# Turning the latents of an attention layer by VectorE blocks and a row exchange instead of TensorE transposes

## The chip, the cores and the metric

One Trainium2 chip; the kernel runs on one of its cores. The metric is the device time of one execution in microseconds (us). A profiled execution gives the span from the first to the last instruction of the program, and the rows that are quoted. PE is TensorE (PEld its weight loads), DVE VectorE, ACT ScalarE, POOL GpSimd, SP SyncE; a trailing q (SPq) marks the engine's instruction queue, where a DMA is issued.

## The reference, cut to what matters

Two layers of an encoder on 512 tokens of width 2048. Of the projection `z` the change touches the first 832 columns: the query latent (512), the key/value latent (256) and the shared rotary key (64).

```python
for l in range(DEPTH):                                   # 2
    h = rmsnorm(x, pre_norm_g[l])
    z = h @ w_in[l]                                      # 2048 -> 4928 columns
    q_lat, kv_lat, k_pe, gb, gc, xin, q_mem, gate = split_cols(z)   # 512, 256, 64, ...
    q  = (rmsnorm(q_lat, q_norm_g[l]) @ w_uq[l]).reshape(b, s, 8, 192)
    q  = concat(q[..., :128], apply_rope(q[..., 128:], cos, sin))
    kv = (rmsnorm(kv_lat, kv_norm_g[l]) @ w_ukv[l]).reshape(b, s, 8, 256)
    k_nope, v = kv[..., :128], kv[..., 128:]
    k  = concat(k_nope, apply_rope(k_pe, cos, sin) for all heads)
    a_out = mla_attention(q, k, v)                       # 8 heads, softmax over 512 tokens
    c_out = short_gated_conv(gb, gc, xin, conv_w[l])
    m_out = memory_attention(q_mem, rmsnorm(mem) @ w_mk, rmsnorm(mem) @ w_mv)   # 4 heads, 256 tokens
    y = concat(a_out, c_out, m_out) * silu(gate)
    x = x + rmsnorm(y @ w_o[l], post_norm_g[l])
```

All arrays are float32.

## The kernel before, in words

**Precision.** TensorE works on float32r operands, each number split in a high and a low part; a product is three matmuls (lines 272 to 274: high by high, high by low, low by high). A weight block of 256 x 512 is loaded by a DMA into one of 8 buffers `wr` (line 146), ScalarE writes its high part `wh` (line 189), VectorE the rest `wl` (line 190). There are three buffers each for `wh` and `wl`, so the two engines are at most three blocks ahead of TensorE.

**The projection** is cut into five groups of columns. Each group is computed by Strassen's rule in seven products (P1 to P7) of halves; their weight operands are sums and differences of blocks. Sums are partly made by VectorE (line 178) and partly by the DMA: POOL issues a load that adds to a buffer already used (`accum_op=add`, line 163 by way of 146). Such a load can only be issued when VectorE has written the `wl` that was made from the buffer's earlier content, and the next `wh` of that buffer waits until it has landed.

The fourth group gives the latents. The fifth, `g4`, gives the gates of the attention heads and has 28 steps of 12 matmuls each: 0 to 3 are P1, 4 to 11 P5 and P2 in turn, 12 to 19 P6 and P3, 20 to 23 P7, 24 to 27 P4. The weight block of step 23 is that of step 19 with another block added to it by a POOL load. What follows `g4` is the mixer: rotary queries first, then the memory heads, then the eight attention heads.

**Order.** TensorE, SP and POOL run in the order in which the program is written; the order of ScalarE and VectorE is made by a scheduler when the kernel is built, and is fixed then. Every engine executes in its order, so a waiting instruction holds all behind it. Work that may be late is put in a queue of deferred functions (`pr.defer`); `pr.until` empties that queue up to a condition.

**The tokens' order.** The host permutes the tokens in x so that a 32 x 32 block transpose on VectorE (line 935) and a set of DMAs that exchange rows between partitions (`exchange`, lines 937 to 943; SBUF to SBUF, 32 partitions each, pieces of 512 bytes) turn a [tokens x columns] array into [columns x tokens] in natural order. The gates and the memory queries go that way: `y<-gm`, `y<-ga`, `y<-cy` on SP's queue and `QmL<-qm` on POOL's.

**The latents** do not. While `g4` runs, `latents_begin` (line 1044) normalises them in place (ScalarE squares, POOL takes the root, VectorE multiplies). After step 16, `latent_turn` (line 1077) is woven into the steps: four TensorE transposes (line 917) into a PSUM bank `tps`, from which ScalarE and VectorE write the high and low parts `cqH`, `cqL` and `ckv` (lines 277 and 278). There are six such groups in each layer, between steps 16 and 23. The rotary key goes by TensorE as well (`k_rope_turn`, line 1068, tiles `krps`). Queries and keys stay in the permuted order of tokens, so the product with the gate puts the result back in place with strided views (line 1268).

Of the kernel before, what the change touches and what calls it, by code (L numbers as in the profile page):

```python
# [12 lines left out]
P = 128  # L13
# [214 lines left out]
def encoder(tc, x, xt, mem, memt, positions, columns, conv_w, w_in, q_norm_g, w_uq, w_qr, kv_norm_g, w_ukv,  # L228
# [159 lines left out]
    def tables_turned():  # L388
        G["tabd"] = dram.tile([P, 2 * S], F32, name="tabd")
        for n, wide in enumerate(G.pop("wides")):  # L390
            ps = bank("tab")
            for t in range(NT):
                nc.tensor.transpose(ps[:, t * P:(t + 1) * P], wide[:, t * P:(t + 1) * P], G["ident"])
            tab = scrap("tab")
            nc.scalar.copy(tab, ps)
            nc.gpsimd.dma_start(G["tabd"][:, n * S:(n + 1) * S], tab)
# [342 lines left out]
    def projection(l):  # L739
# [40 lines left out]
        def own_lat():  # L780
            two = [slab("lat") for _ in range(2)]
            C["lat"] = [two[t // 2][:, (t % 2) * 1024:(t % 2) * 1024 + 832] for t in range(NT)]

        lat = lambda i, j, tt: C["lat"][2 * i + tt][:, j * 416:(j + 1) * 416]
        skip = lambda i, j, tt: None
# [118 lines left out]

    def mem_fetch():
        for n, k in (("Km", 4), ("Vm", 2)):
            t = slab(n, F32R)
            nc.gpsimd.dma_start(t, G[n + "d"])
            G[n] = t.rearrange("p (s i c) -> p s i c", s=2, i=k)


# [113 lines left out]
    def normalise(views, n, gain, by=None):  # L1025
        junk = scrap("junk", n)
        ssq = small(NT, "ssq4")
        for t, v in enumerate(views):
            nc.scalar.activation(junk, v, AF.Square, accum_out=ssq[:, t:t + 1])
        r = rsqrt_mean(ssq, n, NT)  # L1030
        if by:
            nc.gpsimd.tensor_scalar(r, r, by, None, op0=ALU.mult)

        def times(t, v):
            return lambda: nc.vector.scalar_tensor_tensor(v, v, r[:, t:t + 1], gain, op0=ALU.mult, op1=ALU.mult)
        for t, v in enumerate(views):
            pr.defer(0.7, times(t, v))

# [5 lines left out]
    def latents_begin(l, C):  # L1044
        G["q"] = [v[:, :QR_] for v in C["lat"]]
        G["kv"] = [v[:, O_KV:O_KV + KVR] for v in C["lat"]]
        normalise(G["q"], QR_, G["grow"][0], SC_MLA)
        normalise(G["kv"], KVR, G["grow"][1])
        pr.defer(0.0, lambda: G.update(normalised=l))

    def k_rope(C):
        m = scrap("kpm").rearrange("p (b t s i) -> p b t s i", b=2, t=NT, s=2)
        m1, m2 = m[:, 0], m[:, 1]
        for t in range(NT):
            kp = C["lat"][t][:, O_PE:O_PE + ROPE].rearrange("p (s i) -> p s i", s=2)
            nc.vector.tensor_tensor(m1[:, t], kp, G["cos2"][:, t], op=ALU.mult)
            for s in range(2):
                nc.vector.tensor_tensor(m2[:, t, s, :], kp[:, 1 - s, :], G["sin2"][:, t, s, :], op=ALU.mult)
        nc.vector.tensor_tensor(m1, m1, m2, op=ALU.add)
# [7 lines left out]

    def k_rope_turn():
        kab = slab("KAB", F32R)
        for n, src in enumerate(G["kr"]):  # L1070
            ps = bank("krps", F32R)
            for t in range(NT):
                nc.tensor.transpose(ps[:, t * P:(t + 1) * P], src[:, t].rearrange("p d i -> p (d i)"), G["identr"])
            nc.scalar.copy(kab[:, n * S:(n + 1) * S], ps.bitcast(F32))
        G["KA"], G["KB"] = kab[:, :S], kab[:, S:2 * S]

    def latent_turn(l, tag, j):
        def f():
            if j == 0:
                pr.until(lambda: G.get("normalised") == l)  # L1080
                if tag == "cq":
                    G["cq"] = tuple(slab(n, F32R).rearrange("p (k c) -> p k c", c=S) for n in ("cqH", "cqL"))
                else:
                    both = slab("ckv", F32R).rearrange("p (s k c) -> p s k c", s=2, k=2)
                    G["ckv"] = both[:, 0], both[:, 1]
            views = G["q" if tag == "cq" else "kv"]
            ps = turn4(lambda t: views[t], j)
            H, L = G[tag]
            split_to(H[:, j, :], L[:, j, :], ps)
        return f  # L1090
# [9 lines left out]
    def q_rope_steps(l, g):  # L1100
        st = {}

        def products(n):
            def f(*ops):
                if n == 0:
                    st["w"] = tuple(a.rearrange("p (k s c) -> p k s c", k=4, s=2) for a in ops[0])
                    st["ps"] = []
                hi, lo = st["w"]
                cH, cL = G["cq"]
                ps = bank("qr")  # L1110
                st["ps"].append(ps)
                for k in range(4):
                    mm3(ps, (hi[:, k, n], lo[:, k, n]), (cH[:, k, :], cL[:, k, :]), k == 0, k == 3)
            return f
# [33 lines left out]
    def qkv_steps(l, pair, st):  # L1148
# [9 lines left out]
        def fq(i):  # L1158
            def g(*ch):
# [6 lines left out]
                for j in range(4):  # L1166
                    mm3(ps, (hi[:, j, :], lo[:, j, :]), (cH[:, j, :], cL[:, j, :]), j == 0, j == 3)
                split_to(st["Q"][:, 0, i, :], st["Q"][:, 1, i, :], ps)
            return g

        def fk(i):
            def g(*ch):
# [6 lines left out]
                for j in range(2):  # L1179
                    mm3(ps, (hi[:, j, i * 256:i * 256 + P], lo[:, j, i * 256:i * 256 + P]),  # L1180
                        (cH[:, j, :], cL[:, j, :]), j == 0, j == 1)
                split_to(st["K"][:, 0, i, :], st["K"][:, 1, i, :], ps)
            return g

        def fv(b):
            def g():
# [5 lines left out]
                for i in range(2):  # L1192
                    sl = slice((2 * b + i) * P, (2 * b + i + 1) * P)
                    for j in range(2):
                        mm3(ps[:, i * 256:(i + 1) * 256].rearrange("p (h c) -> p h c", h=2),
                            (cH[:, j, sl], cL[:, j, sl]), (hi[:, j], lo[:, j]), j == 0, j == 1)
                p3 = ps.rearrange("p (i c) -> p i c", i=2)
# [5 lines left out]
    def head_iters(j, rope, src, keys, whole=False):  # L1203
# [50 lines left out]
        def av(b):  # L1254
            def g():
# [7 lines left out]
                if b == 1:  # L1263
                    y = G["ys"][j // 4][:, j % 4, :]
                    if rope is None:
                        nc.vector.tensor_tensor(y, st["o"], y, op=ALU.mult)
                    else:
                        nc.vector.tensor_tensor(in_tiles(y), of_tiles(st["o"]), in_tiles(y), op=ALU.mult)
            return g
# [47 lines left out]
    def mixer(l, C, pair2, tail):  # L1317

        (p0, rotate0, fetch0), (p1, rotate1, fetch1) = (q_rope_steps(l, g) for g in range(2))
        put(p0)  # L1320
        add(lambda: nc.scalar.activation(small(1, "ex"), C["ga0"][:, NT - 1][:, 0, :1], AF.Exp, scale=0.0))
# [201 lines left out]
    for l in range(depth):  # L1523
# [230 lines left out]
```

## Time and profile before

| | |
|---|---|
| median of 3 runs | 1458.38 us (1457.26 to 1458.82) |
| the profiled execution's own time | 1458.55 us |
| its span | 1456.8 us (1.75 us lie around it) |
| PE busy | 1441.9 us, 99% of the span |
| DVE busy, ACT busy | 1109.4 us, 870.0 us |
| granted TensorE clock | 0.998 |
| DMA | 299.48 MB, mean 206 GB/s |

A row of a group or of a timeline names the line, the engine, the operation, out<-in, the shape; then busy time or start and duration. What stands in square brackets is how long the engine was idle just before, and what ended that. In a window's row the number ahead of the last is the mean busy share of the 16 DMA engines (it can go over 1, since packets of one engine overlap); rows of DMA queues give packets, megabytes and that share; q0 is the queue of POOL's DMAs, q1 that of SP's. Layer 0's part of the change lies at 340 to 430 us of the span, layer 1's some 724 us later.

### The profile page before, as it was taken

Reading aid. Unit: us, or ns where it says so; the run is one execution under the profiler, and the core shown is the slowest. Engines: PE = TensorE matmul, PEld = TensorE weight load, DVE = VectorE, ACT = ScalarE, POOL = GpSimd, SP = SyncE. Lnnn points to the kernel's source line nnn. Section 1 sums busy time; section 2 is a strip of 40 time slices with the busy share of each in tenths; the row PEclk is TensorE's granted clock in tenths of the full one; section 3 lists DMA queues with packets and bytes.
Section 4 is the critical chain, followed back from the end, with each engine's and each line's share of the span. In section 5 each row is a group of like instructions: output and inputs, shape, how many; then the busy total and the mean of one; then the engine's idle time right before and its main releaser. Section 6 shows DMA issues by size and latency. Waiting matters only on the chain.

```text
span 1456.8 us, 19495 instructions
## 1 busy us (share of the span) xinstructions
PE 1441.9 (99%) x7008; PEld 1227.6 (84%) x7008; DVE 1109.4 (76%) x1533; ACT 870.0 (60%) x1346; POOL 288.6 (20%) x312
## 2 busy tenths in 40 slices
PE   9999999999999999999999999999999999999997
PEld 8888888899888888888898888778988888888886
DVE  5899685987678788868879666769576776788687
ACT  7856444545559688644777434454465586776543
POOL 0032303031501100311210333030325000004111
PEclk9999999999999999999999999999999999999999
DMA  9999969597976472795987999697979865129973
GB/s 368 415 260 219 232 184 205 138 204 225 242 241 175 123 252 87 142 254 137 334 292 225 233 235 213 193 173 170 204 203 243 245 173 145 31 86 162 271 160 130
DMA packets 162499, 299.48 MB, mean 206 GB/s; under 512 B 12801, under 2 KB 52257, under 8 KB 158561
## 3 DMA queue, kind: packets, MB, share of 16 engines
q0 software_dynamic: 57216, 127.49, 43.1%
q1 hardware_dynamic: 105184, 170.74, 36.5%
q8 instruction: 55, 0.90, 0.2%
q14 instruction: 44, 0.35, 0.1%
HBM read 266.05 MB, written 21.63 MB: 197 GB/s over the span
## 4 chain that ended last, share of the span: by engine, by line
PE 86%; DMA 5%; DVE 4%; issue 3%; POOL 2%; ACT 1%; SPq 0%; POOLq 0%; DVEq 0%; ACTq 0%
PE P L273 20%; PE P L274 20%; PE P L272 20%; DMA wr<-in_w_in_dram 2%; PE ptp L1250 2%; DVE wl L190 2%; POOL wr L146 1%; PE o L273 1%; PE o L272 1%; PE o L274 1%; PE sc L272 1%; PE sc L273 1%; PE sc L274 1%; DMA wr<-in_w_mv_dram 1%; PE qps L274 1%
## 5 line engine op out<-in xcount | busy, mean ns | idle before, releaser
L189 ACT CAST wh<-wr 128x1024 fp32r<-128x1024 f32 (+2 forms) x436 | 444.4, 1023 | 426.7 <-PE P L274 312.0
L190 DVE TENSOR_TENSOR wl<-wr,wh 128x1024 fp32r<-128x1024 f32 (+2 forms) x436 | 514.5, 1184 | 234.8 <-ACT wh L189 232.1
L272 PE MATMUL P<-wh,S 128*128 128x512 f32 (+1 forms) x896 | 345.4, 386 | 1.8 <-DVE qm L542 1.1
L273 PE MATMUL P<-wl,S 128*128 128x512 f32 (+1 forms) x896 | 344.3, 384 | 2.5 <-DVE wl L190 2.3
L274 PE MATMUL P<-wh,S 128*128 128x512 f32 (+1 forms) x896 | 343.8, 384 | 0.0
L272 PE MATMUL P<-wh,A 128*128 128x512 f32 (+1 forms) x656 | 252.6, 385 | 0.0
L273 PE MATMUL P<-wl,A 128*128 128x512 f32 (+1 forms) x656 | 251.7, 384 | 0.5 <-DVE wl L190 0.5
L274 PE MATMUL P<-wh,A 128*128 128x512 f32 (+1 forms) x656 | 251.5, 383 | 0.0
L146 POOL DMA_DIRECT2D wr<-in_w_in_dram x132 | 158.4, 1207 | 419.4 <-DVE wl L190 200.9
L273 PEld LDWEIGHTS P<-wl,S 128*128 128x128 f32 x896 | 168.2, 188 | 34.1 <-DVE wl L190 4.5
L272 PEld LDWEIGHTS P<-wh,S 128*128 128x128 f32 x896 | 168.2, 188 | 33.4 <-ACT wh L189 1.8
L274 PEld LDWEIGHTS P<-wh,S 128*128 128x128 f32 x896 | 168.2, 188 | 30.1
L273 PEld LDWEIGHTS P<-wl,A 128*128 128x128 f32 x656 | 123.2, 188 | 22.5 <-DVE wl L190 0.8
L274 PEld LDWEIGHTS P<-wh,A 128*128 128x128 f32 x656 | 123.1, 188 | 22.2
L272 PEld LDWEIGHTS P<-wh,A 128*128 128x128 f32 x656 | 123.1, 188 | 21.9 <-ACT og L585 0.2
L146 POOL DMA_DIRECT2D wr<-in_w_o_dram x40 | 48.3, 1255 | 299.0 <-DVE wl L190 295.2
L1237 ACT ACTIVATE P<-sc,nm 128x512 f32<-128x512 f32 (+1 forms) x96 | 59.7, 622 | 27.8 <-DVE nm L1234 27.5
L1240 ACT ACTIVATE P<-P,rec 128x512 f32<-128x512 f32 (+1 forms) x96 | 62.1, 660 | 7.0 <-DVE rec L1239 7.0
L1234 DVE TENSOR_REDUCE nm<-sc 128x1 f32<-128x512 f32 (+1 forms) x96 | 56.6, 593 | 10.1 <-PE sc L1232 9.0
L178 DVE TENSOR_TENSOR wr<-wr,wr 128x1024 f32<-128x1024 f32 (+1 forms) x36 | 42.3, 1174 | 5.8 <-DMA wr<-in_w_in_dram 5.4
L1250 PE MATMUL ptp<-identr,P 128*128 128x128 f32 x320 | 46.0, 272 | 0.3 <-ACT P L1240 0.3
L1250 PEld LDWEIGHTS ptp<-identr,P 128*128 128x128 f32 x320 | 38.0, 140 | 6.5 <-ACT P L1240 0.7
(324 smaller groups left out, 2098.9 us busy)
## 6 DMA issues: line engine op xcount, KB each, us to landing
wr<-in_w_in_dram SPq DMA_DIRECT2D x128, 512.0 KB, 5.4
wr<-in_w_in_dram POOLq DMA_DIRECT2D x108, 512.0 KB, 7.4
wr<-in_w_o_dram SPq DMA_DIRECT2D x48, 512.0 KB, 6.5
wr<-in_w_o_dram POOLq DMA_DIRECT2D x40, 512.0 KB, 7.1
wr<-in_w_in_dram SPq DMA_DIRECT2D x32, 416.0 KB, 4.0
wr<-in_w_in_dram POOLq DMA_DIRECT2D x24, 416.0 KB, 6.1
wr<-in_w_mk_dram SPq DMA_DIRECT2D x15, 512.0 KB, 8.8
wr<-in_w_mv_dram SPq DMA_DIRECT2D x15, 512.0 KB, 10.1
```

The costliest lines, as they stand in the source:

```text
L146: engine.dma_start(dst, src, **kw)
L178: nc.vector.tensor_tensor(tiles[a], tiles[a], tiles[b], op=ALU.add)
L189: pin(nc.scalar.copy(hi[:, h], src[:, h]))
L190: pin(nc.vector.tensor_tensor(lo[:, h], src[:, h], hi[:, h].bitcast(F32), op=ALU.subtract))
L272: nc.tensor.matmul(ps, ah, bh, start=first, stop=False, **kw)
L273: nc.tensor.matmul(ps, ah, bl, start=False, stop=False, **kw)
L274: nc.tensor.matmul(ps, al, bh, start=False, stop=last, **kw)
L1234: nc.vector.tensor_reduce(nmax, ps, axis=AX.X, op=ALU.max, negate=True)
L1237: nc.scalar.activation(pt, ps, AF.Exp, bias=nmax, accum_out=tot)
L1240: nc.scalar.activation(pt, pt, AF.Copy, scale=rec)
L1250: nc.tensor.transpose(ps[:, k * P:(k + 1) * P], pt[:, k * P:(k + 1) * P], G["ident"])
```

## The change

The host reorders the columns of `w_in` so that each half of the latents' group carries whole blocks: 384 latent columns and one half of the rotary key. The latents lie in two slabs `lat` in blocks of 32 columns. They are normalised as before, then turned by eight VectorE block transposes of 128 x 384 in each layer. `latents_rows_out` moves the rows: 16 DMAs from the first slab to `D1`, all on SP's queue, and 16 from the second to `D2`, half on SP's and half on POOL's, issued between steps 17 and 22 of `g4`. `latents_split` then makes the high parts in `H1`, `H2` and the low parts in place, in four pieces placed after steps 24 to 27. The six groups of TensorE transposes in each layer are gone; the eight of the rotary key stay. The rotary tables and the rotary key are written in natural order of tokens, and the product with the gate needs no strided view any more. The loads of the memory keys `Km`, of the tables and of the memory values `Vm`, formerly one after another behind step 25, are issued after step 26 (`Km`, tables) and after the first rotary product (`Vm`); in POOL's queue the exchange to `D2` comes ahead of them.

```diff
     def latents_begin(l, C):
-        G["q"] = [v[:, :QR_] for v in C["lat"]]
-        G["kv"] = [v[:, O_KV:O_KV + KVR] for v in C["lat"]]
-        normalise(G["q"], QR_, G["grow"][0], SC_MLA)
-        normalise(G["kv"], KVR, G["grow"][1])
+        a, b = C["lat"]
+        normalise([a[:, :, :12], b[:, :, :4]], QR_, G["grow"][0], SC_MLA)
+        normalise([b[:, :, 4:12]], KVR, G["grow"][1])
+        for t in range(NT):
+            for part in (a, b):
+                pr.defer(0.6, lambda t=t, part=part: blocks_turned(part[:, t, :12]))
         pr.defer(0.0, lambda: G.update(normalised=l))
+
+    def latents_rows_out(k, p, queue, C):
+        def f():
+            if k == 0 and p == 0:
+                C["D"] = slab("D1"), slab("D2")
+            exchange(C["D"][k].rearrange("p (c n) -> p c n", n=S)[:, :3], C["lat"][k][:, :, :12], queue, (p,))
+        return f
+
+    def latents_split(n, C):
+        def f():
+            if n == 0:
+                C["H"] = slab("H1", F32R), slab("H2", F32R)
+            (d1, d2), (h1, h2) = C["D"], C["H"]
+            hi, lo = ((h1[:, :768], d1[:, :768]), (h1[:, 768:1536], d1[:, 768:1536]), (h1[:, 1536:], d2[:, :512]),
+                      (h2[:, :1024], d2[:, 512:1536]))[n]
+            split_to(hi, lo.bitcast(F32R), lo)
...
-        lat = [latent_turn(l, "cq", j) for j in range(4)] + [latent_turn(l, "ckv", j) for j in range(2)] + [k_rope_turn]
-        more = [(f, []) for f in lat[:4] + [qm_split(0, C)] + lat[4:6] + [qm_split(1, C)] + lat[6:]]
-        last = weave(g4[16:], more, 1)
-        put(last[:-2])
-        add(mem_fetch)
-        add(tables_fetch)
-        put(last[-2:])
+        put(g4[16:17])
+        add(lambda l=l: pr.until(lambda: G.get("normalised") == l))
+        beside = {
+            17: [latents_rows_out(0, 0, nc.sync, C)], 18: [latents_rows_out(0, 1, nc.sync, C)],
+            19: [latents_rows_out(0, 2, nc.sync, C)], 20: [latents_rows_out(0, 3, nc.sync, C), qm_split(0, C)],
+            21: [latents_rows_out(1, 0, nc.sync, C), latents_rows_out(1, 1, nc.gpsimd, C)],
+            22: [latents_rows_out(1, 2, nc.sync, C), latents_rows_out(1, 3, nc.gpsimd, C)],
+            23: [qm_split(1, C)], 24: [latents_split(0, C)], 25: [k_rope_turn(C), latents_split(1, C)],
+            26: [mem_fetch("Km", 4), tables_fetch, latents_split(2, C)], 27: [latents_split(3, C)],
+        }
+        for n in range(17, 28):
+            put(g4[n:n + 1])
+            for f in beside[n]:
+                add(f)
```

How the instructions stand on SP, layer 0, from the exchange of the gate `gm` to the weights of the first attention heads (`w_qr`, `w_uq`, `w_ukv`). Before:

```order
L943 DMA y_3361<-gm_1834 32x4x128 x16
L146 DMA wr_3535<-in_w_qr_dram 128x1024
L146 DMA wr_3556<-in_w_uq_dram 128x4x128 x2
L146 DMA wr_3583<-in_w_ukv_dram 128x2x512
L146 DMA wr_3608<-in_w_uq_dram 128x4x128 x2
```

Now:

```order
L943 DMA y_3371<-gm_1834 32x4x128 x16
L943 DMA D_142_3475<-lat_2430 32x3x128 x12
L146 DMA wr_3529<-in_w_qr_dram 128x1024
L943 DMA D_142_3475<-lat_2430 32x3x128 x4
L146 DMA wr_3554<-in_w_uq_dram 128x4x128 x2
L943 DMA D_143_3476<-lat_2431 32x3x128 x4
L146 DMA wr_3581<-in_w_ukv_dram 128x2x512
L943 DMA D_143_3476<-lat_2431 32x3x128 x4
L146 DMA wr_3607<-in_w_uq_dram 128x4x128 x2
```

Twenty-four exchange DMAs (`D_142` is `D1`, `D_143` is `D2`) now stand between `gm` and the weights, or among them.

On ACT, layer 0, around the weight blocks of steps 22 (`wr_3274`, now `wr_3279`) to 25 (`wr_2889`) of `g4`. Before:

```order
L189 CAST wh_3537<-wr_3274 128x1024
L277 CAST cqH_3448<-tps_3528 128x512
L792 ACTIVATE ga_117_3039<-ga_117_3039 128x16x32 x2
L189 CAST wh_3559<-wr_3315 128x1024
L189 CAST wh_3585<-wr_2871 128x1024
L277 CAST ckv_3575<-tps_3576 128x512
L189 CAST wh_3611<-wr_2889 128x1024
```

Now:

```order
L189 CAST wh_3531<-wr_3279 128x1024
L791 ACTIVATE ga_117_3039<-ga_117_3039 128x16x32 x2
L277 CAST H_145_3654<-D_142_3475 128x768
L189 CAST wh_3557<-wr_3325 128x1024
L277 CAST H_145_3654<-D_142_3475 128x768
L189 CAST wh_3583<-wr_2871 128x1024
L189 CAST wh_3610<-wr_2889 128x1024
```

Though the program has the first piece of the split behind step 24, the scheduler has put its ScalarE half ahead of the weight block of step 23 (`wr_3325`).

On DVE, layer 0, where the latents are normalised beside steps 3 and 4 of `g4` (`wl_3067`, and `wl_3110`, now `wl_3117`). Before:

```order
L1035 SCALAR_TENSOR_TENSOR lat_2430<-lat_2430,r_3090,growq_3040 128x512
L190 TENSOR_TENSOR wl_3067<-wr_2942,wh_3066 128x1024
L1035 SCALAR_TENSOR_TENSOR lat_2430<-lat_2430,r_3090,growq_3040 128x512
L1035 SCALAR_TENSOR_TENSOR lat_2431<-lat_2431,r_3090,growq_3040 128x512
L190 TENSOR_TENSOR wl_3110<-wr_2871,wh_3109 128x1024
```

Now:

```order
L190 TENSOR_TENSOR wl_3067<-wr_2942,wh_3066 128x1024
L1035 TENSOR_TENSOR ssq_123_3083<-ssq_123_3083,ssq_124_3088 128x4
L1090 TENSOR_TENSOR kpm_3248<-lat_2430,cos_2692 128x4x32
L1091 TENSOR_TENSOR kpm_3248<-lat_2431,sin_2664 128x4x32
L1090 TENSOR_TENSOR kpm_3248<-lat_2431,cos_2692 128x4x32
L1041 SCALAR_TENSOR_TENSOR lat_2430<-lat_2430,r_3096,growq_3040 128x12x32 x4
L190 TENSOR_TENSOR wl_3117<-wr_2871,wh_3116 128x1024
```

A sum of two partial square sums, and four multiplications instead of three, now stand ahead of the `wl` of step 4.

More of the change, by code (lines that the diff above doesn't have):

```diff
@@ L394, in tables_turned @@
             tab = scrap("tab")
-            nc.scalar.copy(tab, ps)
+            nc.scalar.copy(in_tiles(tab), of_tiles(ps))
             nc.gpsimd.dma_start(G["tabd"][:, n * S:(n + 1) * S], tab)
@@ L780, in own_lat @@
         def own_lat():
-            two = [slab("lat") for _ in range(2)]
-            C["lat"] = [two[t // 2][:, (t % 2) * 1024:(t % 2) * 1024 + 832] for t in range(NT)]
-        lat = lambda i, j, tt: C["lat"][2 * i + tt][:, j * 416:(j + 1) * 416]
+            C["lat"] = [slab("lat")[:, :13 * P].rearrange("p (g t j) -> p t g j", t=NT, j=32) for _ in range(2)]
+        lat = lambda i, j, tt: C["lat"][j][:, 2 * i + tt]
         skip = lambda i, j, tt: None
@@ L903, in mem_reload, with mem_fetch @@
         G.setdefault("mT", []).append(two)
-    def mem_fetch():
-        for n, k in (("Km", 4), ("Vm", 2)):
+    def mem_fetch(n, k):
+        def f():
             t = slab(n, F32R)
@@ L1025, in normalise, with times @@
     def normalise(views, n, gain, by=None):
[L1026 to L1030, printed above, removed]
+        junk = scrap("junk", n).rearrange("p (g j) -> p g j", j=32)
+        gain = gain.rearrange("p (g j) -> p g j", j=32)
+        sums = []
+        for part in views:
+            ssq = small(NT, "ssq4")
+            for t in range(NT):
+                nc.scalar.activation(junk[:, :part.shape[2]], part[:, t], AF.Square, accum_out=ssq[:, t:t + 1])
+            sums.append(ssq)
+        if len(sums) == 2:
+            nc.vector.tensor_tensor(sums[0], sums[0], sums[1], op=ALU.add)
+        r = rsqrt_mean(sums[0], n, NT)
         if by:
             nc.gpsimd.tensor_scalar(r, r, by, None, op0=ALU.mult)
[L1034 to L1037, printed above, removed]
+        def times(t, v, g):
+            return lambda: nc.vector.scalar_tensor_tensor(v, v, r[:, t:t + 1], g, op0=ALU.mult, op1=ALU.mult)
+        at = 0
+        for part in views:
+            g = gain[:, at:at + part.shape[2]]
+            at += part.shape[2]
+            for t in range(NT):
+                pr.defer(0.6, times(t, part[:, t], g))
     def latents_rows(l):
@@ L1053, in k_rope @@
         m1, m2 = m[:, 0], m[:, 1]
[L1054 to L1058, printed above, removed]
+        kp = [part[:, :, 12] for part in C["lat"]]
+        for s in range(2):
+            nc.vector.tensor_tensor(m1[:, :, s], kp[s], G["cos2"][:, :, s], op=ALU.mult)
+            nc.vector.tensor_tensor(m2[:, :, s], kp[1 - s], G["sin2"][:, :, s], op=ALU.mult)
         nc.vector.tensor_tensor(m1, m1, m2, op=ALU.add)
@@ L1066, in k_rope, with k_rope_turn @@
         G["kr"] = krA, krB
[L1068 to L1077, printed above, removed]
-        def f():
[L1079 to L1089, printed above, removed]
+    def k_rope_turn(C):
+        def f():
+            G["KA"], G["KB"] = (C["H"][1][:, c * S:(c + 1) * S] for c in (2, 3))
+            for src, dst in zip(G["kr"], (G["KA"], G["KB"])):
+                ps = bank("krps", F32R)
+                for t in range(NT):
+                    nc.tensor.transpose(ps[:, t * P:(t + 1) * P], src[:, t].rearrange("p d i -> p (d i)"), G["identr"])
+                nc.scalar.copy(in_tiles(dst), of_tiles(ps.bitcast(F32)))
         return f
@@ L1112, in f @@
                 for k in range(4):
-                    mm3(ps, (hi[:, k, n], lo[:, k, n]), (cH[:, k, :], cL[:, k, :]), k == 0, k == 3)
+                    mm3(ps, (hi[:, k, n], lo[:, k, n]), (cH[k], cL[k]), k == 0, k == 3)
             return f
@@ L1264, in g @@
                     y = G["ys"][j // 4][:, j % 4, :]
[L1265 to L1268, printed above, removed]
+                    nc.vector.tensor_tensor(y, st["o"], y, op=ALU.mult)
             return g
@@ L1319, in mixer @@
         (p0, rotate0, fetch0), (p1, rotate1, fetch1) = (q_rope_steps(l, g) for g in range(2))
-        put(p0)
+        put(p0[:1])
+        add(mem_fetch("Vm", 2))
+        put(p0[1:])
         add(lambda: nc.scalar.activation(small(1, "ex"), C["ga0"][:, NT - 1][:, 0, :1], AF.Exp, scale=0.0))
@@ L1736 @@
     given = {n: np.asarray(inputs[n]) for n in _INS}
+    order = np.r_[0:384, 768:800, 384:768, 800:given["w_in"].shape[2]]
+    given["w_in"] = given["w_in"][:, :, order]
     given.update(
```

15 lines of the change are left out of this document (12 added, 3 removed).

## Prediction

> **What bounds the kernel now.** First the page's busy times, then the waits of PE.
>
> ```profile
> PE 1441.9 (99%) x7008; PEld 1227.6 (84%) x7008; DVE 1109.4 (76%) x1533; ACT 870.0 (60%) x1346; POOL 288.6 (20%) x312
> PE P L273 <- DVE wl L190: 2.8, 4, 0.8
> ```
>
> TensorE is busy 99% of the span. Read alone, that says: whatever leaves PE is time won. Whether this holds where the transposes stand is read from the stage itself. The groups of the transposed latents, then PE's timeline in layer 0 (start, duration):
>
> ```profile
> L917 PE MATMUL tps<-identr,lat x48: 270/272/273, 394.2 to 1136.8; 128*128 128x128 f32 x48
> 384.63 0.39 PE L272 MATMUL P<-wh,S 128*128 128x512 f32 x1
> 387.35 0.39 PE L272 MATMUL P<-wh,S 128*128 128x512 f32 x1
> 394.16 0.60 PE L917 MATMUL tps<-identr,lat 128*128 128x128 f32 x4
> 397.36 0.60 PE L917 MATMUL tps<-identr,lat 128*128 128x128 f32 x4
> ```
>
> A step of 12 matmuls takes 387.35 - 384.63 = 2.72 us; with a group of four transposes it takes 397.36 - 394.16 = 3.20. So a group costs PE 0.48 us, the twelve groups 5.8 us. That is the most that the removal can give.
>
> Now step 23, the last of P7, ahead of which the sixth group stands: what ACT, DVE and PE wait for, layer 0 and then layer 1.
>
> ```profile
> 410.48 2.01 ACT L189 CAST wh<-wr 128x1024 fp32r<-128x1024 f32 x2 [3.92 <-DMA wr<-in_w_in_dram]
> 411.56 1.23 DVE L190 TENSOR_TENSOR wl<-wr,wh 128x1024 fp32r<-128x1024 f32 x1 [2.93 <-ACT wh L189]
> 413.58 0.39 PE L273 MATMUL P<-wl,S 128*128 128x512 f32 x1
> ...
> 1136.08 2.00 ACT L189 CAST wh<-wr 128x1024 fp32r<-128x1024 f32 x2 [5.95 <-DMA wr<-in_w_in_dram]
> 1137.15 1.23 DVE L190 TENSOR_TENSOR wl<-wr,wh 128x1024 fp32r<-128x1024 f32 x1 [4.95 <-ACT wh L189]
> 1138.43 0.50 PE L273 MATMUL P<-wl,S 128*128 128x512 f32 x1 [0.76 <-DVE wl L190]
> ```
>
> ACT has idled 3.92 us in layer 0, 5.95 us in layer 1, until the adding POOL load of step 23's block landed (410.4 and 1136.0). DVE finishes its `wl` at 411.56 + 1.23 = 412.79 and 1138.4. PE starts the matmul that reads it at 413.58, 0.79 us later, in layer 0; in layer 1 PE is already waiting. All six groups of transposes lie ahead of this point, so their time is cover for the load: without them PE would come 2.9 us earlier and find nothing. What can be won is 0.79 us in layer 0 and nothing in layer 1.
>
> Why does the load land so late? The stage's DMA:
>
> ```profile
> 401.36 1.21 POOL L146 DMA_DIRECT2D wr<-in_w_in_dram  x1 [1.89 <-DVE ga L542]
> 394.00:410.00 16.00, 16.00 (x81) 13.19 (x80) 11.82 (x15) 9.11 (x12) 4.73 (x5) 1.00 1.12 237
> q0 software_dynamic: 630, 1.21, 112.1%
> ```
>
> It is issued at 401.36 and takes 9 us. From 394 to 410 the DMA engines are busy at 1.12. In 396 to 402, with q0 alone, its 630 packets also make 112%: that is the ceiling. The stage is bound by DMA, not by PE.
>
> **The change part by part.** *Removed*: the transposes (above; worth 0.79 us), six splits on ACT and DVE. *Added on the DMA engines*: in each layer 32 exchange DMAs of 3 x 32 = 96 pieces of 512 bytes; `D1`'s 16 are 1536 packets. The nearest rows are the exchanges of the gates, 128 packets each: `y<-ga` where nothing else runs (453 to 459 us), `y<-gm` in this very stage, both with the median from issue to landing, then `gm`'s issue on SP in each layer.
>
> ```profile
> q1 hardware_dynamic: 1255, 0.57, 37.0%
> y<-ga SPq DMA_DIRECT2D x10, 64.0 KB, 2.0
> y<-gm SPq DMA_DIRECT2D x16, 64.0 KB, 6.5
> 375.35 16.00 SPq L943 DMA_DIRECT2D y<-gm  x16
> 1100.23 16.83 SPq L943 DMA_DIRECT2D y<-gm  x16
> 399.89 0.35 SPq L146 DMA_DIRECT2D wr<-in_w_qr_dram  x1
> ```
>
> 1255 packets fill 37.0% of 16 engines for 6 us: 0.028 us of one engine each. `D1`'s 1536 take 1536 x 0.028 / 16 / 1.12 = 2.4 us of the full DMA stage; that is what they can at most push the adding load back. But their own arrival is worse, since the two queues share. The queues' rows at 410.5 to 413.5, then at 1118 to 1121:
>
> ```profile
> q0 software_dynamic: 158, 1.16, 96.2%
> q1 hardware_dynamic: 158, 0.08, 13.0%
> ...
> q0 software_dynamic: 247, 0.49, 96.4%
> q1 hardware_dynamic: 286, 0.13, 17.5%
> ```
>
> 158 packets against 158: the engines take one packet of each queue in turn, whatever its size. Against adding loads of 2 KB packets q0 makes 247 / 3 = 82 packets a us and q1 82 to 95. `D1` starts behind `gm`, whose last issue ends at 375.35 + 16.00 = 391.35, so its packets flow from about 395 (an issue to landing takes 6.5 us there). 1536 packets at 82 to 95 a us are 16.2 to 18.7 us; `w_qr`, which stands among them as before (399.89), brings 128 packets of 4 KB, 1.6 us. `D1` is complete at 412.8 to 415.3; I take 414.0. In layer 1 `gm`'s issue ends 1117.06 - 391.35 = 725.7 us later: 1139.7.
>
> *Moved into the way*: ACT's cast of `D1`'s first piece now stands ahead of step 23's `wh`, and DVE's `wl` behind that. ACT holds the queue until `D1` is whole. The cast lies between these, by size:
>
> ```profile
> L277 ACT CAST A<-X 128x1024 fp32r<-128x1024 f32 x6 | 6.1, 1039 | 0.0
> L277 ACT CAST cqH<-tps 128x512 fp32r<-128x512 f32 x8 | 4.6, 580 | 2.3 <-PE tps L917 2.3
> ```
>
> 768 columns: about 0.81 us. From a landed block to the end of its `wl` it is 412.79 - 410.48 = 2.31. So the `wl` of step 23 ends 0.81 + 2.31 = 3.1 us behind `D1`: at 417.1 in layer 0 instead of the 413.58 that PE needed (+3.5), at 1142.8 in layer 1 instead of 1138.43 (+4.4). Together **+7.9 us**. The adding load itself, 410.4 + 2.4 = 412.8 at the latest, is then no longer the last. The ends of this term: the cast meets a `D1` that is already there, and the load is not pushed: 412.79 and 1138.43, -0.8 us in all. Load pushed by 2.4, `D1` early: +1.6 and +2.4, 4.0 in all. I am nearer to the upper end because `gm`, same size, same queue, same stage, takes 6.5 us a DMA.
>
> The Trainium skill prices it otherwise: its page "DMA: Bandwidth & Descriptors", section "Anatomy of one DMA", gives a DMA about 2.0 us plus its bytes by 436 GB/s, so 2.1 us for 48 KB (an estimate from that page). By that `D1` would be there near 404 and rival A below would hold. The 2.0 us of `y<-ga` agree, alone; the 6.5 us of `y<-gm` do not.
>
> *Added on DVE*, beside steps 3 to 12: eight block transposes of 384, and the normalisation in twelve pieces for eight. The rows of the nearest kinds, and POOL's and DVE's times at the start of it:
>
> ```profile
> L935 DVE STREAM_TRANSPOSE ga<-ga 128x512 f32<-128x512 f32 x16 | 11.0, 700 | 1.0 <-ACT ga L792 0.8
> L1035 DVE SCALAR_TENSOR_TENSOR lat<-lat,r,growq 128x512 f32<-128x512 f32 x8 | 5.8, 743 | 0.3
> L1035 DVE SCALAR_TENSOR_TENSOR lat<-lat,r,growk 128x256 f32<-128x256 f32 x8 | 3.5, 472 | 0.0
> 351.25 0.19 POOL L282 TENSOR_SCALAR ms<-ssq 128x4 f32<-128x4 f32 x1 [12.46 <-ACT junk L1029]
> 353.09 0.75 DVE L1035 SCALAR_TENSOR_TENSOR lat<-lat,r,growq 128x512 f32<-128x512 f32 x1
> 356.22 1.21 DVE L190 TENSOR_TENSOR wl<-wr,wh 128x1024 fp32r<-128x1024 f32 x1
> 371.01 1.23 DVE L190 TENSOR_TENSOR wl<-wr,wh 128x1024 fp32r<-128x1024 f32 x1 [1.50 <-ACT wh L189]
> ```
>
> Transposes: 8 x about 0.5 = 4 us. The multiplications stay about level (by 1.06 ns a column 0.61, 0.34 and 0.47 for 384, 128 and 256: 5.7 us, before 4.9), and four rope products replace twelve. The four squares more on ACT put the root off by about 3 us (351.25 to 354.4; from there to the first multiplication it is 353.09 - 351.25 = 1.84, so 356.2), and four multiplications of 0.53 now stand ahead of step 4's `wl`, so it ends at about 359.6 instead of 357.4. PE needs it at 394.16 - 13 x 2.72 = 358.8: about 0.9 us of waiting, which the 2.9 us freed ahead of step 23 cover. By 371 DVE has gaps of 1.50 us per step again. I cost this at nothing; uncovered it is 0.9 us a layer, and if the adding loads and `gm` start later for it, up to 1.6 a layer.
>
> *`D2`, the loads and the end of the stage.* Each exchange DMA on SP waits for the landing of the eighth before it, so `D2`'s last lands 2.0 to 6.5 us after 414, by 420.5. ACT and DVE hold the `wh` and `wl` of step 26 for it, some 3.6 us of work; PE, itself late, needs that at 417.1 + 3 x 2.72 = 425.3. It fits by 1.2 us: nothing. `Km`, the tables and `Vm` are later, but `D2` takes their place in the DMA stage, and they are read in the mixer, past the rotary products. The splits read SBUF in four pieces for six: no more time than now.
>
> The sum is made against the profiled execution: 1458.55 (its span 1456.8 and 1.75 around it; 0.2 over the median of the runs, 1458.38). 1458.55 + 7.9 = 1466.4, so **1466 us**.
>
> **The rivals.** *A: the exchange is hidden*, `D1` there by 409, the load pushed little: -0.8 to +2.4 us, 1457.8 to 1461. For it: `y<-ga` at 2.0 us. Against: the full DMA stage. *B: PE is the bound and gets its 5.8 us*: 1452.8. For it: 99% busy. Against: the two waits at step 23; it needs the adding load to land 2 us earlier while more is moved. *C: a second wait*. If `D2` is complete only after 421.7, step 26 waits too, and each us beyond is a us of each layer; with 3 us each, or the late start of the normalisation (1.6 each), 1470 to 1478. For it: eight more issues on SP behind waits, and weights among them. Against: POOL's adding loads are through by then. The Trainium skill's main page ("Trainium Kernel Development and Optimization", section "Key Constraints") says that DMAs of several queues run on the same 16 engines, so that spreading saves only issue time; the 158 against 158 agree, and `D2`'s second queue is no help in C.
>
> **How the numbers follow.** Forecast 0.62 (1461 to 1470), A 0.20, B 0.05, C 0.13. What can be told from no change here is 0.2%, 2.9 us. Slower: forecast and C, 0.75. Same: A less a little, 0.19. Faster: B and a little of A, 0.06. The range leaves out B, the lower half of A and the upper half of C, some 2 in 10: 1459.5 to 1473.5.
>
> **What would show it.** Right: no `tps`; PE's largest gap of the stage at step 23, put down to `wl`; ACT's cast of `H1` idle before by 4 us or more and ended by the DMA `D1<-lat`; landing of `D` about 6 us or over. Wrong: that cast without a wait; PE without a gap from 390 to 425; or the gap at step 26 (C) or step 4.

## The result, and the profile after

The changed kernel takes 1477.28 us (median of 4 runs, 1475.87 to 1479.08). Run beside it on the same chip, the kernel before took 1458.60 us. The ratio is 1.0127, with a 95% interval of 1.0109 to 1.0145. It is slower, as forecast, but by 18.7 us where 7.9 were forecast; 1477.3 lies above the range (1459.5 to 1473.5). The profiled execution took 1478.31 us, its span is 1476.5 us: 19.7 us longer than the span before.

The page's busy times after the change, then what PE waited for (total us, times, longest):

```profile
PE 1441.6 (98%) x6960; PEld 1223.7 (83%) x6960; DVE 1117.1 (76%) x1539; ACT 871.4 (59%) x1358; POOL 297.0 (20%) x328
...
PE P L272 <- ACT wh L189: 15.3, 2, 7.7
PE P L272 <- ACT ga L585: 3.6, 2, 2.1
```

48 matmul rows fewer (the transposes), and yet PE's busy time has hardly changed (1441.9 us before): part of it is now the same matmuls, only slower. Two new lines stand in the waits: 15.3 us for `wh`, one long wait in each layer, and 3.6 us for `ga` of line 585, also one in each layer.

**Step 23.** PE's timeline after the change, layer 0 and layer 1:

```profile
419.87 0.80 PE L272 MATMUL P<-wh,S 128*128 128x512 f32 x1 [7.66 <-ACT wh L189]
421.12 0.80 PE L273 MATMUL P<-wl,S 128*128 128x512 f32 x1 [0.46 <-DVE wl L190]
421.72 0.63 PE L274 MATMUL P<-wh,S 128*128 128x512 f32 x1
422.14 0.63 PE L272 MATMUL P<-wh,S 128*128 128x512 f32 x1
423.42 0.46 PE L272 MATMUL P<-wh,S 128*128 128x512 f32 x1
427.85 0.50 PE L272 MATMUL P<-wh,A 128*128 128x512 f32 x1 [1.43 <-ACT ga L585]
986.39 0.42 PE L272 MATMUL P<-wh,S 128*128 128x512 f32 x1
1153.31 0.79 PE L272 MATMUL P<-wh,S 128*128 128x512 f32 x1 [7.62 <-ACT wh L189]
1154.57 0.80 PE L273 MATMUL P<-wl,S 128*128 128x512 f32 x1 [0.46 <-DVE wl L190]
1157.29 0.46 PE L273 MATMUL P<-wl,S 128*128 128x512 f32 x1
1162.14 0.50 PE L272 MATMUL P<-wh,A 128*128 128x512 f32 x1 [2.12 <-ACT ga L585]
```

The same matmuls in PE's timeline before:

```profile
414.73 0.40 PE L272 MATMUL P<-wh,S 128*128 128x512 f32 x1
417.47 0.39 PE L272 MATMUL P<-wh,A 128*128 128x512 f32 x1
976.72 0.50 PE L272 MATMUL P<-wh,S 128*128 128x512 f32 x1 [0.65 <-ACT wh L189]
1139.93 0.40 PE L273 MATMUL P<-wl,S 128*128 128x512 f32 x1
1142.44 0.39 PE L272 MATMUL P<-wh,A 128*128 128x512 f32 x1
```

Each row has its counterpart: the matmul of step 23 that reads `wl`, then one five or six matmuls on, then the one that now waits for `ga`. From these rows, and the two of step 23 that the prediction shows (413.58, 1138.43), the lateness of PE splits up:

| | layer 0 | layer 1 | sum | forecast |
|---|---|---|---|---|
| `wl` matmul of step 23 (layer 1 less the 9.7 us it arrives with, 986.39 - 976.72) | +7.5 | +6.5 | 14.0 | 7.9 |
| the matmuls behind it, slower | +1.1 | +1.2 | 2.4 | none |
| the wait for `ga`, inside step 24 | +1.7 | +2.3 | 4.0 | none |

That is 20.4 us; 0.7 of layer 0's are given back before 977 us, and 19.7 are left. So there are three things to explain: a `D1` that comes later than reckoned, a slow PE behind the wait, and a second wait.

**ACT's queue**, at step 23 and at the second wait, with DVE's `wl` of step 23:

```profile
418.04 0.83 ACT L277 CAST H<-D 128x768 fp32r<-128x768 f32 x1 [8.92 <-DMA D<-lat]
418.77 1.04 ACT L189 CAST wh<-wr 128x1024 fp32r<-128x1024 f32 x1
419.85 1.23 DVE L190 TENSOR_TENSOR wl<-wr,wh 128x1024 fp32r<-128x1024 f32 x1 [8.21 <-ACT wh L189]
426.69 0.62 ACT L277 CAST H<-D 128x512 fp32r<-128x512 f32 x1 [2.43 <-DMA D<-lat]
427.21 0.58 ACT L585 COPY ga<-P 128x512 f32<-128x512 f32 x1
...
1151.48 0.83 ACT L277 CAST H<-D 128x768 fp32r<-128x768 f32 x1 [8.84 <-DMA D<-lat]
```

The forecast picture: ACT idles for 8.92 us until `D1` is whole, and the weights of step 23 stand behind. But `D1` is whole at 418.0, not 414.0; in layer 1 at 1151.5, not at 1139.7 + 9.7 = 1149.4. And some 9 us later the same happens with `D2`. This time the instruction behind the cast is ACT's copy of P7's second PSUM bank (line 585), and PE needs that bank in the middle of step 24.

**Why `D1` is late.** SP's queue after the change, layer 0 and 1:

```profile
376.71 0.37 SPq L146 DMA_DIRECT2D wr<-in_w_in_dram  x1
377.13 18.19 SPq L943 DMA_DIRECT2D y<-gm  x16
395.42 13.42 SPq L943 DMA_DIRECT2D D<-lat  x12
411.11 2.85 SPq L943 DMA_DIRECT2D D<-lat  x4
1110.72 18.23 SPq L943 DMA_DIRECT2D y<-gm  x16
1129.06 15.24 SPq L943 DMA_DIRECT2D D<-lat  x12
```

`gm`'s issue ends at 377.13 + 18.19 = 395.32 instead of 391.35, and in layer 1 at 1128.95 instead of 1117.06 + 9.7 = 1126.7. So it is 4.0 and 2.2 us late, and `D1` stands behind it. From there to a whole `D1` it takes 22.7 and 22.5 us; the prediction's own numbers make 414.0 - 391.35 = 22.7. The way of `D1` as a whole was sized rightly. Its start was not.

`gm` starts 1.8 us later in layer 0 because a weight load stands ahead of it on SP (376.71), and that load waits until DVE has read its buffer. DVE's rows, after the change and then before it:

```profile
356.71 2.23 DVE L1041 SCALAR_TENSOR_TENSOR lat<-lat,r,growq 128x384 f32<-128x384 f32 x4 [1.26 <-POOL r L1038]
374.55 1.02 DVE L935 STREAM_TRANSPOSE lat<-lat 128x384 f32<-128x384 f32 x2
375.51 1.18 DVE L190 TENSOR_TENSOR wl<-wr,wh 128x1024 fp32r<-128x1024 f32 x1
```

```profile
373.68 1.22 DVE L190 TENSOR_TENSOR wl<-wr,wh 128x1024 fp32r<-128x1024 f32 x1 [1.45 <-ACT wh L189]
```

The normalisation starts 3.6 us later than before (356.71 against 353.09), because POOL's root `r` is late, and the block transposes come on top: from there DVE has no gap until this `wl`, which ends at 376.69 instead of 374.90. SP goes on at 376.71. The other 2.2 us are in the issuing itself, 18.2 us instead of 16.0: `gm`'s DMAs now take 7.2 us each from issue to landing, 6.5 before. In layer 1 the start is 0.8 us late and the issuing 1.4 us longer.

**The slow PE.** Windows of PE after the change; behind the busy time stand the granted clock, the DMA share and GB/s:

```profile
416.00:420.00 4.00, 0.13 (x1) 0.59 1.01 334
420.00:422.00 2.00, 1.54 (x3) 0.50 1.02 274
422.00:424.00 2.00, 2.00 (x7) 0.61 0.57 195
```

The granted clock falls to one half in the wait and stays there until about 423.4, 3.5 us after PE has work again. Matmuls follow each other every 0.43 us (421.72, 422.14) instead of every 0.23.

### The profile page after: what moved, and what is told of

Its sections match the earlier page's. It is cut to its first block, busy times and chain, and to the rows that moved or that the text cites. A ratio compares the mean times of both kernels' runs of the same rounds, so it can differ in the third digit from the quotient of the medians.

```text
span 1476.5 us, 19530 instructions
## 1 busy us (share of the span) xinstructions
PE 1441.6 (98%) x6960; PEld 1223.7 (83%) x6960; DVE 1117.1 (76%) x1539; ACT 871.4 (59%) x1358; POOL 297.0 (20%) x328
## 4 chain that ended last, share of the span: by engine, by line
PE 82%; DMA 6%; issue 5%; DVE 2%; POOL 2%; SPq 2%; ACT 1%; POOLq 0%; DVEq 0%; ACTq 0%
PE P L273 19%; PE P L272 19%; PE P L274 19%; DMA wr<-in_w_in_dram 2%; PE ptp L1269 2%; SPq L943 1%; DMA D<-lat 1%; PE o L273 1%; PE o L274 1%; PE o L272 1%; DVE wl L190 1%; PE sc L272 1%; PE sc L273 1%; PE sc L274 1%; POOL wr L146 1%
## 5 line engine op out<-in xcount | busy, mean ns | idle before, releaser
L189 ACT CAST wh<-wr 128x1024 fp32r<-128x1024 f32 (+2 forms) x436 | 444.0, 1023 | 426.7 <-PE P L274 296.9
L272 PE MATMUL P<-wh,S 128*128 128x512 f32 (+1 forms) x896 | 345.8, 386 | 16.3 <-ACT wh L189 15.3
L273 PEld LDWEIGHTS P<-wl,A 128*128 128x128 f32 x656 | 123.2, 188 | 22.5 <-DVE wl L190 0.9
```

The lines of the kernel that those rows point to most:

```text
L189: pin(nc.scalar.copy(hi[:, h], src[:, h]))
L272: nc.tensor.matmul(ps, ah, bh, start=first, stop=False, **kw)
L273: nc.tensor.matmul(ps, ah, bl, start=False, stop=False, **kw)
```

## The experiments

The theory, in letters of the expectations: **L**, `D1` comes late, and **O**, the order of ACT's queue turns that into a wait of PE; **C**, a long wait halves PE's clock; the traffic itself costs little. The rivals: the traffic costs the time whoever waits for it (D, and S for the DMA stage as a whole), the early work on DVE does (E), PE is the bound (P), or the wait only moves when its cause is taken away (M). Ratios are to runs of the kernel before on the same chip.

### What the parts cost: three kernels in which nothing waits for the exchange

The first leaves the exchange out:

```diff
 # latents_rows_out
-            exchange(C["D"][k]..., C["lat"][k][:, :, :12], queue, (p,))
 # latents_split: from the slabs of lat instead of D
-            split_to(hi, lo.bitcast(F32R), lo)
+            src = ...                        # the same columns of the two slabs of lat
+            split_to(hi, lo.bitcast(F32R), src)
```

> The changed kernel without its 32 exchange DMAs a layer: the splits take the VectorE-turned slabs as they stand, so the latents are turned within blocks of 32 only (this part of the computation is left out). Everything else, all DVE and ACT work included, stays. Theory L (late exchange: D1 lands late, ACT's cast of it holds step 23's wh, D2 a second wait): nothing is left to wait for at step 23 but the adding load; the time falls to 1457 to 1461. Rival E (the early part: late root, block transposes and squares in DVE's and ACT's way): it stays at 1468 or above. Rival P (PE is the bound, it gets the 5.8 us of the transposes): 1452 to 1454.

The second has the same splits, but `exchange` writes into two other slabs, `E1` and `E2`:

> As the kernel without the exchange, but the 32 exchange DMAs a layer are issued as in the changed kernel, at the same places on SP and POOL, into two slabs that nothing reads; the splits still take the slabs turned by VectorE only (the exchange between blocks stays left out of the result). Theory L: the load alone pushes the adding loads by at most the 2.7 us a layer seen in the changed kernel; 1460 to 1465. Rival D (the DMA traffic itself costs the time, whoever waits for it): 1474 to 1478, as the changed kernel.

The third is the kernel before without the transposes:

```diff
 # latent_turn of the kernel before
-            ps = turn4(lambda t: views[t], j)
-            split_to(H[:, j, :], L[:, j, :], ps)
+            split_to(H[:, j, :], L[:, j, :], views[j])     # the key/value latents likewise, in halves
...
```

> The kernel before without its 48 transposes of the latents: the splits read the normalised slabs, not turned (this part of the computation is left out). All other work stays where it is. Theory L with the prediction's term (the transposes are cover for the adding load of step 23): 0.8 us won, 1457 to 1458. Rival P (PE is the bound): 5.8 us won, 1452.6.

| kernel | median us | ratio, 95% interval |
|---|---|---|
| before, no transposes | 1459.90 | 1.0021, 1.0009 to 1.0033 |
| changed, no exchange | 1462.79 | 1.0035, 1.0021 to 1.0048 |
| changed, exchange into slabs that nobody reads | 1465.20 | 1.0059, 1.0044 to 1.0074 |
| changed | 1477.28 | 1.0127, 1.0109 to 1.0145 |

Three rivals fall. P: without its transposes the kernel before gains nothing, it loses 0.2%. E, as the whole of the loss: without the exchange the time is 1462.79, not 1468 or above. D: with all 32 DMAs of each layer in flight the time is 12 us below that of the changed kernel (10 by the ratios), so waiting for them is most of the loss. That run lies 0.2 us above the range of L (1460 to 1465), the run without the exchange 1.8 above its own; the early part may cost about 3 us (1462.8 against 1459.9), but the intervals overlap, and that is not settled.

Nor do the exchange's packets show in the adding load of step 23. ACT's row for it in the kernel without the exchange, then POOL's issue of it in the changed kernel:

```profile
415.32 1.04 ACT L189 CAST wh<-wr 128x1024 fp32r<-128x1024 f32 x1 [3.39 <-DMA wr<-in_w_in_dram]
404.19 1.22 POOL L146 DMA_DIRECT2D wr<-in_w_in_dram  x1 [1.36 <-DVE wl L190]
```

Before the change that load was issued at 401.36 and had landed at 410.48. It lands 4.8 us later with no exchange at all, and it is issued 2.8 us later in the changed kernel, where POOL waits for DVE: the lateness is there before the packets can act. The kernel without transposes has the load at 412.85, also without an exchange, so a part of this is not the early part's either.

That removing PE work loses time was expected by nobody. PE in the kernel without transposes, step 23 of layer 0:

```profile
413.95 0.51 PE L272 MATMUL P<-wh,S 128*128 128x512 f32 x1 [2.12 <-ACT wh L189]
415.21 0.51 PE L273 MATMUL P<-wl,S 128*128 128x512 f32 x1 [0.76 <-DVE wl L190]
415.88 0.63 PE L272 MATMUL P<-wh,S 128*128 128x512 f32 x1
```

Here PE waits where it had transposes to do, for 2.1 us and 0.8 us, and in layer 0 its clock is halved behind that; in layer 1 it is not (the last section shows why).

### The order of ACT's queue alone

```diff
+        for s in g4[21:]:
+            for u in s[1]:
+                u.pinned = True          # cast and wl stay in program order
 # latents_split
-            split_to(hi, lo.bitcast(F32R), lo)
+            pr.pin(nc.scalar.copy(hi, lo))
+            pr.pin(nc.vector.tensor_tensor(lo.bitcast(F32R), lo, hi.bitcast(F32), op=ALU.subtract))
```

> The changed kernel, whole, with one thing undone: the casts and subtractions of the weights of steps 21 to 27 and of the four latent splits are kept in the order in which the program writes them, so that ACT's cast of D1 stands behind the weights of step 26 and no longer ahead of those of step 23. Transfers and their order are untouched. Theory O (ACT's order turns a late D1 into a wait of PE; the traffic costs little): PE waits at step 23 for the adding load alone, as in the run whose exchange nobody waits for; 1463 to 1468. Rival M (the wait only moves, to the first rotary products, which need all of D1 and D2): 1471 to 1476.

1465.24 us, ratio 1.0061 (1.0040 to 1.0083): the changed kernel, whole, 12 us faster (10 by the ratios) by the order of ACT's and DVE's instructions. Both waits are gone with it, that for `D1` at step 23 and that for `ga` behind `D2`; the edit does not tell them apart. ACT in this kernel (the profiled execution, 1461.67 us, is the fastest of five):

```profile
413.02 2.95 ACT L189 CAST wh<-wr 128x1024 fp32r<-128x1024 f32 x3 [5.22 <-DMA wr<-in_w_in_dram]
420.73 0.83 ACT L1077 CAST H<-D 128x768 fp32r<-128x768 f32 x1
```

Three weights are cast as soon as the adding load has landed (413.0; before 410.5), and the cast of `D1` comes at 420.73 without any wait. It is the time of the kernel whose exchange nobody waits for, 1465.20. Theory O stands, M falls: a `D1` and a `D2` as late as these cost nothing if nothing urgent is queued behind them.

### The clock

The kernel with kept casts still waits 2.2 and 3.5 us at step 23, for the adding load. The first try to fill that wait put 24 unread transposes between steps 22 and 23 of the kernel without transposes:

```diff
+        def filler():
+            ps = bank("fill")
+            for n in range(24):
+                nc.tensor.transpose(ps[:, n % 4 * P:(n % 4 + 1) * P], <128 columns of the latents>, G["ident"])
```

> The kernel before without the turning of the latents (left out as in the earlier run of that kind), but with 24 transposes a layer, which nobody reads, in one piece between steps 22 and 23, where PE waits. Theory C (a wait of PE of about 3 us and more halves its clock for some 3.4 us after it, which costs another 1.7 us; work in the wait keeps the clock): 2.9 us of extra work a layer make the kernel 2 to 4 us faster than the same kernel without them, 1456 to 1458. Rival (the loss of that run is the adding loads' alone): no gain from the filling, 1459 to 1463.

1463.36 us, 1.0050 (1.0033 to 1.0068): slower than unfilled, against theory C. But its trace shows a wait that the edit brought with it: PE stands for 1.44 us in each layer, inside step 24 (the next expectation calls it step 26), until ACT has copied the second bank. The scheduler had put a gate's activation ahead of that copy. PE's clock was 1.00 throughout. So the run told nothing of C, and was repeated with the two copies kept together:

> The filled kernel again (the kernel before without the turning of the latents, which is left out; 24 unread transposes a layer between steps 22 and 23), with ACT's two copies at the end of P7 kept next to each other, ahead of the first gate's activation, as they stand in the kernel without filling: the first filled run had them apart, and step 26 waited 1.7 us a layer for the second. Theory C (PE's clock is halved for about 3.4 us by a wait of 3 us or more): the clock stays at 1.00 in every 2 us of the stage, and with step 26's wait gone the kernel lies at 1456 to 1458.5, at or below the 1459.9 of the one without filling. Rival: the filling gains nothing, 1459.5 to 1462.

1459.67 us, 1.0016 (1.0002 to 1.0030), against 1.0021 (1.0009 to 1.0033) unfilled: no difference that can be measured. It is above the range of theory C and in that of its rival, though the clock stayed at 1.00. The same filling in the changed kernel with kept casts, and then its control without the filling:

> The changed kernel, whole, with the casts kept in program order as in the run of that kind (1465.2), ACT's two copies at the end of P7 kept together, and 24 unread transposes a layer between steps 22 and 23, which is the 2.9 us of PE work that the change took away. Theory C: PE's wait at step 23 falls from 3.9 and 5.2 us to 1 and 2.3 us, its clock is never halved there, and the time falls by the slow stretch of about 1.7 us in a part of the runs: 1462 to 1464.5, with a smaller spread than the 1461.7 to 1468.6 seen. Rival: extra work on PE costs or changes nothing, 1465 to 1468.

> The control of the filled kernel: the changed kernel, whole, casts kept in program order and ACT's two copies kept together, everything as there but without the 24 unread transposes. Its instructions on ACT stand as in the first kernel with kept casts (1465.2). Theory C (a long wait of PE at step 23 halves its clock, and the filling prevented that): 1464 to 1467, above the 1461.4 of the filled one, with the clock below 1.00 behind step 23 in at least one layer. Rival (filling is worth nothing, the two runs differed by chance): 1460 to 1463.

Filled 1461.39 us, 1.0033 (1.0019 to 1.0046); not filled 1464.88, 1.0061 (1.0045 to 1.0077). Behind step 23, in layer 0 and then layer 1, first unfilled, then filled:

```profile
416.00:420.00 4.00, 3.31 (x8) 0.59 0.96 306
1140.00:1144.00 4.00, 2.76 (x6) 0.54 1.06 286
```

```profile
416.00:420.00 4.00, 3.24 (x15) 1.00 1.04 329
1140.00:1144.00 4.00, 3.23 (x13) 1.00 0.80 275
```

2.9 us of useless work a layer make the kernel 3.5 us faster, with intervals that only touch. The filled kernel lies 0.6 us below the range of theory C, its control inside it; the smaller spread that C expected did not come (7.5 us against 6.9). For this kernel C is supported; for the one without transposes, where in the trace one layer of two had lost its clock, the gain was too small to be seen.

### Other places for the DMAs

The changed kernel with `D1` and `D2` in `gm`'s place on SP and `gm` behind step 27; then the same with the casts kept; then the kernel without transposes with `gm` behind step 27:

```diff
         put(g4[12:13])
-        add(gate_rows(3, "gm", C))
+        add(lambda l=l: pr.until(lambda: G.get("normalised") == l))
+        # D1 behind steps 13 and 14, D2 behind 15 and 16, all on nc.sync
...
-            26: [...], 27: [latents_split(3, C)],
+            26: [...], 27: [latents_split(3, C), gate_rows(3, "gm", C)],
```

> The changed kernel with the order on SP turned round: D1 and D2 (all 32 on SP) take gm's place behind steps 13 to 16, the 16 gm exchanges follow after step 27. Nothing is left out. Theory L: D1 lands near 397 instead of 418, D2 near 412 instead of 426, no wait for either; what is left is the adding loads' push of about 2 us a layer: 1459 to 1464. Rival D (traffic): 3072 packets stand where 2048 of gm and 1536 of D1 stood, the time stays at 1473 to 1478. Rival W (the next-stage weights, now behind 32 exchanges on SP, become the wait): 1466 to 1474, with a gap of PE in the first rotary products after step 27.

> The changed kernel, whole, with both: D1 and D2 take gm's place on SP behind steps 13 to 16 and gm follows behind step 27, and the casts of steps 21 to 27 and of the splits are kept in program order. Theory O: no wait for D1 or D2 is left on ACT ahead of step 28; 1462 to 1467, no more than with the order of the casts alone. Rival M: the second wait of the version with the exchange first (D2 near 418, ahead of step 24) moves to the rotary products; 1470 to 1475.

> The kernel before without the turning of the latents (left out), and with the 16 gm exchanges moved from behind step 12 to behind step 27, where the DMA engines have room. Theory S (the stage is bound by its DMA traffic): 2048 packets fewer let the adding loads land up to 3.2 us earlier, PE no longer waits long enough at step 23 to lose its clock, and the transposes' time is won: 1452 to 1455. Rival Q (the adding loads go at the pace of their own queue): 1458 to 1462, as without the move.

1475.09 us (1.0126, 1.0111 to 1.0141), 1474.22 (1.0121, 1.0102 to 1.0139) and 1459.83 (1.0023, 1.0009 to 1.0038). None of the three gains of theories L, O and S came, though each first step of them did. The times lie in the ranges of the rivals D, M and Q: for D that is luck, since the traces show other waits, and M named the rotary products where the wait is in the softmax behind them. With the exchange first, ACT no longer waits for `D1`. Its row for `D2`, and two of PE's waits in that kernel:

```profile
418.07 1.56 ACT L277 CAST H<-D 128x512 fp32r<-128x512 f32 x2 [3.41 <-DMA D<-lat]
```

```profile
PE P L272 <- ACT wh L189: 5.5, 3, 3.0
PE ptp L1269 <- ACT P L1259: 5.1, 2, 2.6
```

The scheduler now puts the casts of `D2`, presumably because it takes `D2` for early, ahead of step 24's weights: the wait has moved. And a wait of 2.6 us a layer is new in the mixer (`ptp`), also with the casts kept; in that second kernel the clock is halved behind it in both layers. In all three kernels DVE has the rotary products (`rm`) between the softmax's reductions, where in the others they are through before; the trace of the third shows it:

```profile
446.21 0.39 PE L272 MATMUL sc<-Km,QmH 128*128 128x256 f32 x1 [1.47 <-DVE rm L1133]
```

There the waits at step 23 had fallen to 0.5 us for `wh` and 0.8 for `wl`, with the clock at 1.00, as S says; the mixer, with this wait in each layer, took it back. The last kernel tested that: the filled one with `gm` in the mixer, ahead of the rotation, which leaves the rotary products first.

> The filled kernel (whole, casts kept, 24 unread transposes) with the 16 gm exchanges moved from behind step 12 into the mixer, ahead of the first rotation, so that D1 and D2 go first on SP and the rotary products on DVE stay ahead of the softmax's reductions (where gm stood directly behind step 27, they fell behind them and PE waited in the mixer). Theory S (traffic: 2048 packets leave the stage, the adding loads of P7 land 1 to 2 us earlier, D1 near 397): 1457.5 to 1460.5. Rival Q (the exchange's 3072 packets stand in gm's place, the adding loads land no earlier): 1461 to 1464. Rival X (the mixer waits again, gm or the loads behind it): 1465 to 1472.

1463.52 us, 1.0047 (1.0035 to 1.0059); with `gm` in its old place 1461.39. The mixer's wait is mostly gone (1.3 us are left of 5.1), but nothing is won: rival Q. ACT's row for the adding load of step 23 with `gm` in its old place, and then with `gm` in the mixer:

```profile
414.67 2.96 ACT L189 CAST wh<-wr 128x1024 fp32r<-128x1024 f32 x3 [5.36 <-DMA wr<-in_w_in_dram]
415.57 2.95 ACT L189 CAST wh<-wr 128x1024 fp32r<-128x1024 f32 x3 [5.17 <-DMA wr<-in_w_in_dram]
```

The load lands no earlier. Nor is `D1` whole near 397: after twelve of its DMAs, SP's queue stands for 10 us behind `w_qr` (issued at 400.89), and the last four of `D1` come after that. No version tested beats the kernel before.

## Why the prediction was right or wrong

**PE is not the bound at step 23: right.** The transposes were cover for the adding load. Taking them away alone wins nothing (1459.90).

**ACT holds step 23 for `D1`: right**, shown by undoing the order of the queues (10 to 12 us, the second wait included). From `D1` whole to the end of `wl` it takes 419.85 + 1.23 - 418.04 = 3.04 us, forecast 3.1. The sign named for it was a gap of PE put down to `wl`; the trace puts 7.66 us to `wh` and 0.46 to `wl`, which is the same chain. The adding load's push, forecast from the packets of `D1` at 2.4 at most, is 413.02 - 410.48 = 2.5 with kept casts. That agrees by luck: it is 4.8 us without an exchange, so the packets are not needed for it.

**`D1` whole at 414.0 and 1139.7: the step that failed.** The term was sized with "`D1` starts behind `gm`, whose last issue ends at 391.35", taken from the profile of before as if the change left it there. It ends at 395.32, and 2.2 us late in layer 1. The span grew by 19.7 us where 7.9 were forecast; of the 11.8 between them this is 6.1 (14.0 against 7.9). The late start itself had been foreseen and priced, "up to 1.6 a layer", and then set to nothing, because the 2.9 us freed on PE would cover it and DVE would have gaps again by 371. DVE has none until 376.69, and that cover is PE's. The chain here does not go through PE: the late root and the block transposes hold a `wl` on DVE, that holds a buffer, the buffer's load holds `gm` on SP, and `gm` holds `D1`. This chain is read from the rows; no run undoes it alone.

**`D2` costs nothing ("it fits by 1.2 us"): wrong.** `D2` is whole at 426.7, not by 420.5. The reckoning looked at the weights of step 26 behind it and passed over ACT's copy of a PSUM bank, which PE needs in step 24: 4.0 us. This is rival C's second wait at another place. C's range, 1470 to 1478, holds the result, though C alone is not what happened.

**Missing altogether: the clock.** A wait was priced at its length. Behind a wait as long as this one PE runs at half clock: 2.4 us here. The Trainium skill has the rule (page "TensorE: Matmul & The Clock Gate", section "Part 1: The HAM clock gate"): the clock drops to half after an idle window of about 3.4 us, in windows that run free of the kernel, and returns after as much sustained work. The return agrees, 3.5 us from 419.87 to 423.4; so do the windows, but they need not be wholly idle (last section).

Rival A (hidden exchange) is refuted by the 8.9 us of ACT's wait, rival B by the kernel without transposes.

## What to carry to other kernels

Before work is taken off an engine that waits further on, look for what that wait ends on, and whether the work was only filling it; a gap of some us may cost more than itself. Where a scheduler fixes the order of an engine's queue in advance, a late transfer holds all that was put behind its reader: keep urgent instructions ahead of such a reader, which here was worth 10 to 12 us, more than any move of the transfers. And when a transfer's arrival is reckoned from the queue in front of it, the queue has to be reckoned anew with the change: each thing in it, and the buffer that each thing waits for.

## What the runs showed of the hardware that was not expected

The clock is lost behind waits shorter than that page's 3.4 us, and not always. Of the ten waits for `wh` at step 23 of 2.0 to 2.7 us (a further 0.5 to 0.8 us for `wl` following), eight halved it. In layer 1 of the kernel without transposes (2.2 us) and in layer 0 of the first kernel with kept casts (2.2 us) it stayed at 1.00.

The traces tell the two cases apart, for they record when the granted clock changes. In each of the 14 traces, counted from the first change, every later one comes after a whole number of windows of 3.413 us. In the changed kernel it falls at 416.72 and again at 1150.58, 215 windows later. Each stretch at half clock inside the program lasts one, two or three windows. Here is the kernel without transposes, cut along its own windows, layer 0 and then layer 1 (PE's busy time, granted clock, DMA share, GB/s):

```profile
412.25:415.66 3.41, 0.95 (x3) 1.00 1.07 408
415.66:419.08 3.42, 3.42 (x10) 0.50 1.05 372
1132.46:1135.88 3.42, 1.91 (x9) 1.00 1.12 300
1135.88:1139.29 3.41, 1.94 (x7) 1.00 1.08 409
1139.29:1142.70 3.41, 3.15 (x14) 1.00 1.05 361
```

In layer 0 the wait lies in one window, with PE busy for 0.95 us of it, and the next window runs at half clock. In layer 1 a wait of the same length lies across two windows, 1.91 and 1.94 us remain busy in them, and the clock stays. This holds in all 14 traces: every full-clock window with PE busy for 1.59 us or less by the profile was followed by half clock (32 of them, the programs' ends included; the one with 1.59 is in layer 0 of the last kernel, from 408.69), and none with 1.62 us or more was. So what counted was about half of a fixed window, and where a wait of 2 to 3 us falls in it is chance. The unread transposes count as work: in seven of the eight layers filled, the window that holds most of them has only 0.6 to 1.6 us of other work, and the clock stayed.
